# Six query/key blocks between the early wide blocks, a fifth step by seven products in each of these, and the two recurrences side by side, in a hybrid decoder block on one Trainium2 core

## The chip, the cores and the metric

The kernel runs on one core of a Trainium2 chip. The engines that matter here are TensorE (PE, with the loading of its stationary operand shown apart as PEld), VectorE (DVE), ScalarE (ACT), GpSimd (POOL) and SyncE (SP). POOL and SP issue transfers here and do little else. The metric is the time of one execution on the device, in microseconds; the time of a kernel is the median of its runs.

## The reference

One decoder layer over 256 positions of width 2048, all in float32. What is computed:

```python
a = rmsnorm(h, norm_mix_pre)
q_a, k_a, v_a, q_r, f_r, i_r, g_r, gate_a, gate_r = split_columns(a @ w_in)   # 17408 columns
# attention: rotary on q and k, 3 groups (dilations 1, 4, 16) x 8 heads of 128,
# the groups mixed per position by their softmax denominators
attn = ...                                              # 256 x 1024
# recurrence: f = lb + (1 - lb) * sigmoid(f_r); S_t = diag(f_t) S_{t-1} + (1 - f_t) i_t^T;
# o_t = S_t^T silu(q_r_t); RMSNorm per head, times silu(g_r)
r_out = ...                                             # 256 x 1024
y = sigmoid(gate_a) * (attn @ w_attn_branch) + sigmoid(gate_r) * (r_out @ w_hgrn_branch)
h = h + rmsnorm(y @ w_mix_out, norm_mix_post)
gt, up = split(rmsnorm(h, norm_ffn_pre) @ w_ffn_gate_up)
h = h + rmsnorm((silu(gt) * up) @ w_ffn_down, norm_ffn_post)
```

## The kernel before, in words

**Products.** Every float32 operand is split into a high part (ACT copies it to a shorter format) and a low part (DVE subtracts the high part from the operand). A float32 product is then three TensorE products: high by high, high by low, low by high. The weights are streamed from memory once, in units of 1 MB.

**Blocks and steps.** The matrix products are cut into blocks, a block into steps; `seq` is the list of all steps and the main loop (L1833 ff.) emits it in that order. There are three kinds of block:

- A **wide** block (`Wide`, `multiply_wide`) has two times 512 columns and eight steps. A plain step is 24 matmuls of 512 columns. In a step **by seven products** the two-by-two block product is made from seven products in the manner of Strassen, 21 matmuls instead of 24. It costs other engines more: POOL's queue adds a second piece of weights onto the loaded one (L304), DVE makes sums of pieces (`sum`, L405 and L406), ACT their high part (`dh`, L416) and DVE their low part (`dl`, L419). All steps need ACT's high part `w` (L391) and DVE's low part `wl` (L411). After the last step by seven, `gather` (L523 to L532) and `add_up` (L541) put the side products together. The activations' own sums (`pair_sums`, kept as `so`, one for each entry of `X7`) are made once.
- A **W** block has 256 columns, the columns on the rows of the result; four steps of 16 matmuls, half of them 512 and half 256 columns wide. The 24 query and key blocks are of this kind. Their steps need the split at L356 (ACT) and L357 (DVE). When a block has ended, `both_halves` (L274 on ACT, L276 on DVE) takes the result out of its two banks, and `evac_rope` turns it (two rows of L974, then L981 and L982) into a slot `qk`.
- An **N** block is used for the first gate, the branch products and the first FFN block.

**Strings.** `EARLY` holds one string for each of the ten early wide blocks (gates, values, recurrence inputs); an 8 is a plain step, a 7 a step by seven. `EARLY` "87878787" has four sevens.

**Order.** The order of instructions on each engine is that in which the program writes them (a manual schedule): `ahead(n)` writes the split of step n + 2, then come the matmuls of step n, then `advance(evacs)` one piece of the evacuation in work, and `advance_lanes()` one piece of each lane. A lane is a queue of small pieces: the recurrence (two halves of four heads, each eight levels, with `kk` and `fq` products of 8 matmuls on TensorE) and the eight attention heads. An engine does not overtake: an instruction that waits holds all that is written behind it on its engine.

**Slots.** Three slots each for `w` and `wl`, one for `sum`, `dh` and `dl`; three for `raw` (four in some ranges). PSUM has four banks called `acc` and four called `aux`. In the early stage a wide block takes them as two pairs of each: its plain results stand in two pairs of one side, the side products in two pairs of the other, and `FLIP` changes the sides from block to block. In the middle (query/key blocks) a W block takes two single `acc` banks and the lanes take `aux`.

The few lines of the loop that set the order:

```python
        if n >= 2:
            rest = ahead(n)
...
            multiply_wide(st)
...
        advance(evacs)
...
        advance_lanes()
        if type(b) is Block and b.kind == 'W' and n % 5 == 0:
            advance(lanes[1])
```

## Time and profile before

| | us |
|---|---|
| median of 3 runs | 1680.43 |
| lowest and highest | 1678.48, 1681.29 |
| span of the profiled execution, first to last instruction | 1678.2 |
| PE busy in it | 1667.2 (99%) |
| DVE busy | 1452.9 (87%) |
| ACT busy | 950.4 (57%) |

The profiled execution gives its time as its span; the medians of runs lie 2.2 us above it, since a run counts also what lies around the first and the last instruction. In a row of groups the columns are line, engine, operation, output and inputs, their shapes, count, busy time, mean time of one in ns, and idle time of the engine just before them with what ended it. In a timeline row they are start, duration, engine, line, operation, count. Matmuls are pipelined, so that their duration (390 ns for 512 columns) is longer than their spacing: what one costs is read from start to start.

### The profile page before, as it was taken

To read this page: it belongs to the slowest core of one execution; us is meant where nothing else is said; L and a number is where in the kernel's file an instruction comes from. 1 tells how busy PE (TensorE), PEld (TensorE's weight loads), DVE (VectorE), ACT (ScalarE), POOL (GpSimd) and SP (SyncE) were. 2 spreads that over 40 slices of the span, in tenths; PEclk is the share of its full clock that TensorE was granted. 3 is DMA by queue.
4 is the path that set the end of the run, shared out by engine and by line. 5 is a ranking of instruction groups with operands and counts; after the bars stand their busy time and mean duration, and the time that the engine had idled before them with its cause. 6 is when DMAs were issued, how large, how long until landed. Compare 5 with 4: busy or idle time off the path is not lost.

```text
span 1678.2 us, 21503 instructions
## 1 busy us (share of the span) xinstructions
PE 1667.2 (99%) x8046; PEld 1393.7 (83%) x8046; DVE 1452.9 (87%) x1487; ACT 950.4 (57%) x951; POOL 233.6 (14%) x319
## 2 busy tenths in 40 slices
PE   9999999999999999999999999999999999999997
PEld 7888888888888888888888888888888888888886
DVE  6798898889889798877668888999999999899988
ACT  6565555556643544354445565666666666666664
POOL 0011111110133143332200010111111111000100
PEclk9999999999999999999999999999999999999999
DMA  8888888877889899999948857999988999887893
GB/s 280 270 261 257 254 259 259 253 246 226 244 268 308 238 310 297 314 258 299 272 159 257 259 179 249 271 273 278 277 275 277 275 273 278 254 257 241 253 306 104
DMA packets 234841, 434.98 MB, mean 259 GB/s; under 512 B 15312, under 2 KB 65536, under 8 KB 234736
## 3 DMA queue, kind: packets, MB, share of 16 engines
q1 hardware_dynamic: 193616, 337.55, 59.8%
q0 software_dynamic: 38496, 90.13, 23.5%
q10 hardware_dynamic: 2624, 5.92, 1.1%
q8 instruction: 63, 1.03, 0.2%
q14 instruction: 42, 0.34, 0.1%
HBM read 420.44 MB, written 52.43 MB: 282 GB/s over the span
## 4 chain that ended last, share of the span: by engine, by line
PE 85%; DVE 6%; DMA 5%; issue 2%; ACT 1%; SPq 0%; DVEq 0%; ACTq 0%
PE acc L170 52%; PE aux L170 31%; DMA raw<-in_w_in 5%; DVE wl L411 3%; DVE e L541 1%; DVE dl L419 1%; PE aux L1019 0%; DVE sum L406 0%; ACT w L391 0%; DVE e L532 0%; DVE sum L405 0%; PE acc L1512 0%; DVE fz L1644 0%; PE aux L640 0%; PE aux L1512 0%
## 5 line engine op out<-in xcount | busy, mean ns | idle before, releaser
L391 ACT ACTIVATE w<-raw 128x2048 fp32r<-128x2048 f32 x220 | 420.7, 1913 | 231.9 <-issue 83.5
L411 DVE TENSOR_TENSOR wl<-raw,w 128x2048 fp32r<-128x2048 f32 x220 | 501.5, 2286 | 22.2 <-ACT w L391 20.0
L170 PE MATMUL acc<-xT,w 128*128 128x512 f32 (+1 forms) x1536 | 279.3, 339 | 0.0
L356 ACT ACTIVATE w<-raw 128x1024 fp32r<-128x1024 f32 (+1 forms) x159 | 166.6, 1051 | 171.4 <-PE acc L170 130.0
L357 DVE TENSOR_TENSOR w<-raw,w 128x1024 fp32r<-128x1024 f32 (+1 forms) x159 | 193.3, 1216 | 80.9 <-ACT w L356 80.0
L170 PEld LDWEIGHTS acc<-xT,w 128*128 128x128 f32 x1536 | 234.0, 188 | 32.5
L416 ACT ACTIVATE dh<-sum 128x1536 fp32r<-128x1536 f32 x107 | 159.5, 1491 | 165.6 <-PE acc L170 58.4
L419 DVE TENSOR_TENSOR dl<-sum,dh 128x1536 fp32r<-128x1536 f32 x107 | 187.5, 1752 | 23.3 <-ACT dh L416 23.2
L170 PE MATMUL acc<-w,xT 128*128 128x512 f32 x602 | 180.8, 392 | 0.3 <-DVE w L357 0.2
L170 PE MATMUL acc<-w,hT 128*128 128x512 f32 x504 | 152.9, 391 | 0.0
L170 PE MATMUL aux<-w,xT 128*128 128x512 f32 x426 | 138.3, 389 | 0.0
L170 PEld LDWEIGHTS acc<-w,xT 128*128 128x128 f32 x602 | 112.2, 188 | 24.8 <-DVE w L357 1.5
L170 PE MATMUL aux<-w,hT 128*128 128x512 f32 x368 | 122.9, 390 | 0.0
L170 PEld LDWEIGHTS acc<-w,hT 128*128 128x128 f32 x504 | 94.0, 188 | 19.7 <-DVE w L357 0.4
L304 POOL DMA_DIRECT2D raw<-in_w_ffn_gate_up x48 | 42.3, 881 | 377.4 <-DMA raw<-in_w_ffn_gate_up 221.3
L170 PEld LDWEIGHTS aux<-w,xT 128*128 128x128 f32 x426 | 80.0, 188 | 16.5
L170 PE MATMUL aux<-w,a 128*128 128x512 f32 x260 | 83.4, 389 | 0.0
L170 PE MATMUL aux<-wl,xT 128*128 128x512 f32 x213 | 83.1, 390 | 0.0
L170 PEld LDWEIGHTS aux<-w,hT 128*128 128x128 f32 x368 | 69.1, 188 | 14.4
L304 POOL DMA_DIRECT2D raw<-in_w_in x37 | 32.7, 884 | 345.8 <-DMA raw<-in_w_in 240.7
L170 PE MATMUL acc<-wl,xT 128*128 128x512 f32 x205 | 80.0, 390 | 0.3 <-DVE wl L411 0.2
L170 PE MATMUL aux<-w,so 128*128 128x512 f32 x198 | 77.1, 389 | 0.0
(341 smaller groups left out, 3028.1 us busy)
## 6 DMA issues: line engine op xcount, KB each, us to landing
raw<-in_w_in SPq DMA_DIRECT2D x271, 512.0 KB, 6.3
raw<-in_w_ffn_gate_up SPq DMA_DIRECT2D x176, 512.0 KB, 5.0
raw<-in_w_ffn_down SPq DMA_DIRECT2D x88, 512.0 KB, 5.7
sum<-ready SPq DMA_DIRECT2D x25, 768.0 KB, 6.6
ready<-in_w_ffn_gate_up POOLq DMA_DIRECT2D x72, 256.0 KB, 6.9
raw<-in_w_mix_out SPq DMA_DIRECT2D x32, 512.0 KB, 5.3
ready<-ready POOLq DMA_DIRECT2D x50, 256.0 KB, 6.9
raw<-in_w_ffn_gate_up POOLq DMA_DIRECT2D x48, 256.0 KB, 6.0
```

The source lines that it names most:

```text
L170: nc.tensor.matmul(ps, lhsT, rhs, start=start, stop=stop, skip_group_check=True)
L304: nc.gpsimd.dma_start(raw[:, :512], rows, accum_op=OP.add)
L356: nc.scalar.activation(wh[:, k], raw[:, k], AF.Copy)
L357: nc.vector.tensor_sub(wl[:, k], raw[:, k], wh[:, k].bitcast(F32))
L391: nc.scalar.activation(hi, raw, AF.Copy)
L411: nc.vector.tensor_sub(lo, raw, hi.bitcast(F32))
L416: nc.scalar.activation(hi, flat, AF.Copy)
L419: nc.vector.tensor_sub(lo, flat, hi.bitcast(F32))
L541: nc.vector.tensor_add(e, b.bank[keys], e)
```

## The change

1. The activations' sums are made for five pairs of row blocks instead of four (`X7`), and six early blocks (numbers 1 to 6 of 0 to 9) have the string "87877877", five steps by seven instead of four.
2. After each of these six blocks stands one W block, the six query/key blocks of head pair 0. Its two results stand in one pair of PSUM (`side`), on the side on which the block before had its side products, and its evacuation is advanced once more at the block's end. Eighteen W blocks remain in the middle.
3. The recurrence's second half is in lane 1 with a wait of 20 pieces (`LAG`), the first stays in lane 0 with a wait of 2; a third lane is added when the first half has ended. Attention of pair 0 is put in the queue at the end of the early stage.
4. The recurrence's outputs go from PSUM to an SBUF slot (ACT) before their squares are taken; two heads of a pair share one PSUM bank for their output; there are 13 slots `f` instead of 16, and three `qk` slots of their own for pairs 0 and 3.
5. Sums of later weights that are made ahead by DMA (`ready_in`) are also issued in the steps of the added W blocks, and the range with a fourth `raw` slot reaches to the end of the early stage.

```diff
-X7, H7 = tuple(range(4)), tuple(range(5))
+X7, H7 = tuple(range(5)), tuple(range(5))
 MIX = [[(3, 0), (4, 0), (5, 0), (0, 1), (6, 0), (1, 1), (2, 0), (7, 0)],
...
-EARLY = [order(x) for x in ["88878878", "87878787", "87878787", "87878787", "87878787", "87878787", "87878787", "87878787", "88787787", "88787878"]]
+EARLY = [order(x) for x in ["88878878"] + ["87877877"] * 6 + ["87878787", "88787787", "88787878"]]
 FFN = [order(x) for x in ["88878787"] + ["87877877", "87877877", "87877877", "87877877", "87877877", "87877877", "87877877", "87877877", "87877877"]]
...
-N_F = 16
+N_F = 13
+BESIDE, LAG = (1, 2, 3, 4, 5, 6), 20
 WIDE_FQ, FLIP = 2, 1
...
         self.steps = nk // self.per
-        self.banks, self.at = None, {}
+        self.banks, self.at, self.side = None, {}, None
...
         return pool["now"].tile([P, 1024], F32, tag="f", bufs=N_F, name=nm(s))
+
+    def kslot(s):
+        return kp.tile([P, 1024], F32, tag="qk", bufs=3, name=nm(s))
...
         if b.banks is None:
-            b.banks = [acc_bank() for _ in range(2)]
+            if b.side:
+                pair = pair_of(b.side)
+                b.banks = [pair[:, n, :] for n in range(2)]
+            else:
+                b.banks = [acc_bank() for _ in range(2)]
         for s in sides:
...
         for half in range(WIDE_FQ):
-            lanes[0].append(waiting(2, recurrence(half)) if half == 0 else recurrence(half))
+            lanes[half].append(waiting((2, LAG)[half], recurrence(half)))
+        start_attention(0)()
...
             if o == 0:
-                qkT[key] = fslot("qk").rearrange("p (h t) -> p h t", h=4)
+                slot = kslot if key[0] in (0, 3) else fslot
+                qkT[key] = slot("qk").rearrange("p (h t) -> p h t", h=4)
             yield
...
-    attnT, recT = [], []
+    attnT, recT, heads_in = [], [], {}
     def attention(pair, hh):
-        o, head = None, 2 * pair + hh
+        head = 2 * pair + hh
         yield
...
             yield
-            if o is None:
-                o = aux()
+            if pair not in heads_in:
+                heads_in[pair] = aux()
+            o = heads_in[pair][:, hh * S : (hh + 1) * S]
             for c in range(4):
...
         hi, lo, _ = attnT[0](head)
-        nc.scalar.activation(hi, o[:, :S], AF.Copy)
-        nc.vector.tensor_sub(lo, o[:, :S], attnT[0].f32(head))
+        nc.scalar.activation(hi, o, AF.Copy)
+        nc.vector.tensor_sub(lo, o, attnT[0].f32(head))
         done.append(head)
...
         ath = at.rearrange("p (h t) -> p h t", h=4)
-        o = [aux(), aux()]
-        for h in range(4):
-            hs = slice(h * P, (h + 1) * P)
-            mm(o[0][:, hs], ath[:, h, :P], v[:, 0, hs], True, True)
-            mm(o[1][:, hs], a2[:, hs], v[:, 0, hs], True, False)
-            mm(o[1][:, hs], ath[:, h, P:], v[:, 1, hs], False, True)
-        yield
+        o = fslot("o").rearrange("p (b c) -> p b c", b=2)
+        for i in range(2):
+            ps = aux()
+            for h in range(4):
+                hs = slice(h * P, (h + 1) * P)
+                if i == 0:
+                    mm(ps[:, hs], ath[:, h, :P], v[:, 0, hs], True, True)
+                    continue
+                mm(ps[:, hs], a2[:, hs], v[:, 0, hs], True, False)
+                mm(ps[:, hs], ath[:, h, P:], v[:, 1, hs], False, True)
+            yield
+            nc.scalar.activation(o[:, i], ps, AF.Copy)
         ss, rr = small("ss"), small("rr")
...
                 nc.scalar.activation(
-                    junk[:, hs], o[i][:, hs], AF.Square,
+                    junk[:, hs], o[:, i, hs], AF.Square,
                     accum_out=ss[:, 4 * i + h : 4 * i + h + 1],
...
                 nc.vector.scalar_tensor_tensor(
-                    out=rt[:, i, hs], in0=o[i][:, hs], scalar=rr[:, 4 * i + h : 4 * i + h + 1],
+                    out=rt[:, i, hs], in0=o[:, i, hs], scalar=rr[:, 4 * i + h : 4 * i + h + 1],
                     in1=g[:, i, hs], op0=OP.mult, op1=OP.mult,
...
                 values_back(half)
+                if half == 0:
+                    lanes.append(deque())
             yield
...
             post=more_x if half == 0 else None)
+    def rope_block(pair, g, o):
+        col, tab = (COL_K, 2) if o else (COL_Q, 0)
+        then = start_attention(pair) if pair and o and g == 2 else None
+        add("W", w_in, KD, col + 1024 * g + 256 * pair, xT,
+            both_halves(evac_rope((pair, g), o, tab, then), 0))
+
+    ropes = [(pair, g, o) for pair in range(4) for g in range(3) for o in (0, 2)]
     early = [(COL_GA, ("a", 0), AF.Sigmoid), (COL_GB, ("r", 0), AF.Sigmoid),
...
                   pre=({0: lambda: advance(evacs), 1: lambda: flush(lanes[1])}).get(n))
+        if n in BESIDE:
+            rope_block(*ropes.pop(0))
+            blocks[-1].side = "acc" if (n % 2 == FLIP) == False else "aux"
     first_w = len(blocks)
...
         add_wide(w_in, KD, COL_QR + 512 * half, xT, evac_qr(half, start_recurrence(half)))
-    for pair in range(4):
-        for g in range(3):
-            for o, col, tab in ((0, COL_Q, 0), (2, COL_K, 2)):
-                then = start_attention(pair) if o and g == 2 else None
-                add("W", w_in, KD, col + 1024 * g + 256 * pair, xT,
-                    both_halves(evac_rope((pair, g), o, tab, then), 0))
+    for x in ropes:
+        rope_block(*x)
     blocks[first_w].pre = end_early
...
     )
+    ready_in |= {st.unit for st in seq if type(st.block) is Block and st.block.side}
     before = sums_before([
...
     wide = [st.unit for st in seq if type(st.block) is Wide]
-    extra.append(range(wide[0] + N_RAW, wide[0] + 8 * len(early), N_RAW + 1))
+    extra.append(range(wide[0] + N_RAW, blocks[first_w].unit0, N_RAW + 1))
     first = blocks[mix_last + 3].unit0 + N_RAW + 1
...
                 evacs.append(b.evac(b.banks))
+                if b.side:
+                    advance(evacs)
             continue
```

Where this moves instructions, in the order in which an engine has them:

VectorE, the join of early blocks 1 and 2, before. `sum_1167` and `wl_1165` belong to the second step of block 2, `wl_1133` to its first, `e_1191` is the gather of block 1:

```order
L411 TENSOR_TENSOR wl_1133<-raw_999,w_1132 128x2048
L405 TENSOR_TENSOR sum_1167<-raw_1033 128x512
L406 TENSOR_TENSOR sum_1167<-raw_1033,sum_1167 128x1024
L530 TENSOR_TENSOR e_1191<-aux_974,e_1191 128x512
L531 TENSOR_TENSOR e_1191<-aux_984,e_1191 128x512
L532 TENSOR_TENSOR e_1191<-e_1191,aux_984 128x1024
L541 TENSOR_TENSOR e_1191<-acc_931,e_1191 128x1024
L541 TENSOR_TENSOR e_1191<-acc_944,e_1191 128x1024
L411 TENSOR_TENSOR wl_1165<-raw_1033,w_1164 128x2048
```

VectorE, the join of blocks 2 and 3 in the change (lines are some eight higher; L361 is the split of a W step, L419 now makes `wl` and L427 `dl`, L280 takes the added W block `acc_1602` out of PSUM, L984 begins its rotation). `wl_1644` and `wl_1672` belong to the first two steps of block 3:

```order
L549 TENSOR_TENSOR e_1587<-aux_1343,e_1587 128x1024
L361 TENSOR_TENSOR w_1595<-raw_1434,w_1595 128x1024
L361 TENSOR_TENSOR w_1622<-raw_1434,w_1622 128x1024
L419 TENSOR_TENSOR wl_1644<-raw_1469,w_1643 128x2048
L413 TENSOR_TENSOR sum_1674<-raw_1504 128x512
L414 TENSOR_TENSOR sum_1674<-raw_1504,sum_1674 128x1024
L419 TENSOR_TENSOR wl_1672<-raw_1504,w_1671 128x2048
L280 TENSOR_TENSOR sum_1697<-acc_1602,sum_1697 128x256 x2
L984 TENSOR_TENSOR w_1708<-sum_1697,tabs 64x512 x2
L427 TENSOR_TENSOR dl_1703<-sum_1674,dh_1702 128x1536
```

The gather is now followed by two W splits, and the two adds that empty the W block's pair stand behind the low parts and sums of two steps of the next wide block.

TensorE at the same place in the change, in the first step of block 3, which follows the W block: its first side of 12 matmuls goes to `acc_1717`, its second to `acc_1730`:

```order
L171 MATMUL acc_1717<-w_1643,xT_111 128x512 x2
L171 MATMUL acc_1717<-wl_1644,xT_111 128x512
L171 MATMUL acc_1717<-w_1643,xT_111 128x512
L171 MATMUL acc_1730<-w_1643,xT_111 128x512
L171 MATMUL acc_1730<-wl_1644,xT_111 128x512
```

`acc_1730` takes the banks of `acc_1602`, so its first matmul, the thirteenth of the step, waits for the second L280 add.

VectorE in the middle, from one `kk` row of the first recurrence on, up to shortly before the next, before:

```order
L1177 TENSOR_TENSOR kk_3624<-kk_3624,tot_3625 128x64x8
L1181 TENSOR_TENSOR tot_3625<-tot_3625 128x64
L1102 COPY_PREDICATED at_3626<-lmask,aux_3976 128x256x2
L357 TENSOR_TENSOR w_4075<-raw_3891,w_4075 128x1024
L974 TENSOR_TENSOR w_4069<-sum_4040,tabs 64x512
L357 TENSOR_TENSOR w_4106<-raw_3891,w_4106 128x1024
L981 TENSOR_TENSOR sum_4040<-sum_4040,tabs 128x512
L982 TENSOR_TENSOR qk_3916<-sum_4040,w_4069 128x512
L1102 COPY_PREDICATED at_3626<-lmask,aux_4097 128x32x16
L1175 TENSOR_TENSOR fq_2999<-fq_2999,tot_3625 128x32x16
L357 TENSOR_TENSOR w_4135<-raw_3954,w_4135 128x1024
```

The same stretch in the change, where `kk_4676`, `x_4707` and `fq_3948` are the second recurrence's:

```order
L1188 TENSOR_TENSOR kk_4251<-kk_4251,tot_4252 128x64x8
L1192 TENSOR_TENSOR tot_4252<-tot_4252 128x64
L1113 COPY_PREDICATED at_4253<-lmask,aux_4604 128x256x2
L1121 TENSOR_TENSOR x_4707<-kk_4676,fq_3948 128x1024
L361 TENSOR_TENSOR w_4712<-raw_4519,w_4712 128x1024
L984 TENSOR_TENSOR w_4702<-sum_4668,tabs 64x512
L361 TENSOR_TENSOR w_4743<-raw_4519,w_4743 128x1024
L991 TENSOR_TENSOR sum_4668<-sum_4668,tabs 128x512
L992 TENSOR_TENSOR qk_4544<-sum_4668,w_4702 128x512
L1113 COPY_PREDICATED at_4253<-lmask,aux_4734 128x32x16
L1186 TENSOR_TENSOR fq_3624<-fq_3624,tot_4252 128x32x16
L1124 TENSOR_TENSOR fq_3948<-fq_3948,fq_3933 128x1024
```

Two rows of 1024 elements, `x_4707` and `fq_3948`, have come between, and nothing has gone; the next `kk` row follows in both after one W split and the two L276 (L280) adds.

## The prediction

> **What bounds the kernel now.** I read the page's busy times first, then a table by stretches (early wide blocks; query/key blocks in two parts; FFN), then what TensorE's weight loads waited for.
>
> ```profile
> PE 1667.2 (99%) x8046; PEld 1393.7 (83%) x8046; DVE 1452.9 (87%) x1487; ACT 950.4 (57%) x951; POOL 233.6 (14%) x319
> 88.00:465.00 377.00, 376.71 (x1674) 310.89 (x1673) 337.66 (x236) 218.12 (x152) 40.36 (x52) 1.00 0.81 251
> 590.00:790.00 200.00, 199.82 (x1246) 177.46 (x1245) 164.73 (x249) 92.20 (x150) 68.26 (x99) 1.00 1.02 297
> 1100.00:1430.00 330.00, 330.00 (x1486) 272.50 (x1485) 304.14 (x234) 203.53 (x138) 34.39 (x39) 1.00 0.90 275
> ```
>
> The stretches' columns are from:to, length, then busy time of PE, PEld, DVE, ACT, POOL, granted clock, DMA share, GB/s. TensorE is busy everywhere at full clock, so a matmul that goes is worth its spacing and every new wait of TensorE is paid in full. VectorE is second: 337.66 of 377 us in the early stage (90%), 304.14 of 330 (92%) in the FFN. How near the early stage is to the edge is shown by these waits:
>
> ```profile
> PEld acc L170 <- DVE wl L411: 1.3, 3, 0.6
> PEld aux L170 <- DVE wl L411: 0.8, 2, 0.4
> 183.32 2.28 DVE L411 TENSOR_TENSOR wl<-raw,w 128x2048 fp32r<-128x2048 f32 x1
> 184.92 0.61 PE L170 MATMUL acc<-w,xT 128*128 128x512 f32 x2
> 185.34 1.92 ACT L391 ACTIVATE w<-raw 128x2048 fp32r<-128x2048 f32 x1
> 185.52 1.75 DVE L419 TENSOR_TENSOR dl<-sum,dh 128x1536 fp32r<-128x1536 f32 x1
> 185.66 0.19 PEld L170 LDWEIGHTS acc<-wl,xT 128*128 128x128 f32 x1 [0.55 <-DVE wl L411]
> 187.19 2.29 DVE L411 TENSOR_TENSOR wl<-raw,w 128x2048 fp32r<-128x2048 f32 x1
> ```
>
> The first two rows are the weight loads' waits between 100 and 465 us: 2.1 us in five waits, all on a low part `wl`. The others are one of them: `wl` ends at 185.60, and the load that wanted it starts at 185.66. It is the low part of a wide block's second step, which stands behind the gather of the block before.
>
> **What is saved.** Six steps change from 24 matmuls to 21: 18 matmuls fewer.
>
> ```profile
> 459.81 0.39 PE L170 MATMUL acc<-wl,xT 128*128 128x512 f32 x1
> 460.49 0.39 PE L170 MATMUL acc<-wl,xT 128*128 128x512 f32 x1
> 461.17 0.39 PE L170 MATMUL acc<-wl,xT 128*128 128x512 f32 x1
> 471.83 21.76 PE L170 MATMUL acc<-xT,w 128*128 128x512 f32 x124
> ```
>
> Every third matmul is of this form, so six spacings are 461.17 − 459.81 = 1.36 us, 227 ns each: 18 × 0.227 = **4.1 us**. The Trainium skill, "TensorE: Matmul & The Clock Gate", section "Back-to-back issue gap", gives about 131 ns for a sustained stream of such pairs; by it the saving would be an estimated 2.4 us. The rows above say 227 ns, so that figure is not used.
>
> The W block gives the gather 11.2 us of cover (64 matmuls at 21.76/124 = 0.1755 us; a step of 16 is 2.81), so the waits of the kind at 185.66 should go from the six joins. In start to start TensorE lost there 185.66 − 185.15 (the second of the pair at 184.92) − 0.23 = 0.28 us for a wait written as 0.55. All five waits at that proportion are 2.1 × 0.28/0.55 = **1.1 us** saved; bounds 0 and 2.1.
>
> The W blocks' own matmuls, splits and rotations are only moved. So are the loads: the raw weights of six W blocks, on SP's queue, in another place. POOL's queue gets six more accumulating pieces of 256 KB.
>
> **The cost at the join.** Reckon from the W block's first matmul as time zero.
>
> ```profile
> L391 ACT ACTIVATE w<-raw 128x2048 fp32r<-128x2048 f32 x70 | 133.9, 1912 | 74.3 <-issue 50.8 <-PE aux L170 12.2 <-PE acc L170 11.1
> L411 DVE TENSOR_TENSOR wl<-raw,w 128x2048 fp32r<-128x2048 f32 x70 | 160.0, 2286 | 1.8 <-ACT w L391 0.6
> L419 DVE TENSOR_TENSOR dl<-sum,dh 128x1536 fp32r<-128x1536 f32 x35 | 61.4, 1753 | 11.0 <-ACT dh L416 11.0
> L406 DVE TENSOR_TENSOR sum<-raw,sum 128x1024 f32<-128x1024 f32 x34 | 41.7, 1225 | 1.2
> L405 DVE TENSOR_TENSOR sum<-raw 128x512 f32<-128x512 f32 x34 | 23.3, 686 | 18.2 <-DMA raw<-in_w_in 17.9 <-DVE wl L411 0.2
> L276 DVE TENSOR_TENSOR sum<-acc,sum 128x256 f32<-128x256 f32 x34 | 12.7, 414 | 0.0
> L541 DVE TENSOR_TENSOR e<-aux,e 128x1024 f32<-128x1024 f32 x10 | 11.8, 1219 | 0.4
> L531 DVE TENSOR_TENSOR e<-aux,e 128x512 f32<-128x512 f32 x5 | 3.5, 692 | 0.5
> L357 DVE TENSOR_TENSOR w<-raw,w 128x1024 fp32r<-128x1024 f32 x70 | 85.5, 1223 | 22.4 <-ACT w L356 21.9
> L974 DVE TENSOR_TENSOR w<-sum,tabs 64x512 f32<-64x512 f32 x32 | 22.0, 686 | 1.0
> ```
>
> There are three `w` slots, so the high part of the next wide block's first step waits for the slot of the W block's second step, free at 2 × 2.81 = 5.62. From there the chain is fixed by the order rows: high part 1.91, `wl` 2.29, the second step's sums 0.69 + 1.23, its `wl` 2.29, and only then the two adds that empty the W block's pair, 0.83. That ends at 14.86. TensorE ends the W block at 11.23, does the wide step's first side (12 × 0.227 = 2.72) and wants the pair at 13.95: a wait of 0.9 us. With the overlap of neighbours in the rows above (wl starts to dl starts 185.52 − 183.32 = 2.20, and 187.19 is ahead of the high part's end at 187.26) the chain is 14.4 and the wait 0.4. A semaphore's way adds some 0.2 to the start. I take 0.7, six times: **4.2 us**; bounds 6 × 0.4 = 2.4 and 6 × 0.9 = 5.4. Queued behind the waiting matmul are only matmuls; behind the L280 adds on VectorE stands the rotation's first pair, 2 × 0.69, and then `dl` of the second step.
>
> Is VectorE late elsewhere in such a stage? A block with five sevens is 8 × 2.29 + 5 × (1.23 + 0.69 + 1.75) + gather and adds 5.0 (0.69 × 2 + 1.22 × 3) = 41.7 us, the W block 4 × 1.22 + 0.83 + 4 × 0.69 = 8.5, together 50.2, less what neighbours overlap (some 25 times 0.08, 2.20 against 2.29), about 48, in 24 × 0.227 × 3 + 21 × 0.227 × 5 + 11.2 = 51.4 us of TensorE: 93%, where the FFN's same string runs at 92% without a wait. So I cost the fifth seven's sums at nothing; the cover is that margin of some 3 us a stage, of which the `w` slot already takes about 2.6 at the join. Without it, up to the fifth seven's own 0.69 + 1.23 + 1.75 = 3.7 us a stage would show.
>
> **The cost in the middle.** With one recurrence and no attention beside it, VectorE and TensorE meet like this:
>
> ```profile
> L1110 DVE TENSOR_TENSOR x<-kk,fq 128x1024 f32<-128x1024 f32 x2 | 2.4, 1216 | 0.0
> L1113 DVE TENSOR_TENSOR fq<-fq,fq 128x1024 f32<-128x1024 f32 x2 | 2.4, 1220 | 0.0
> 518.44 0.69 DVE L1177 TENSOR_TENSOR kk<-kk,tot 128x512 f32<-128x512 f32 x1
> 519.83 1.89 PE L170 MATMUL aux<-fq,kk 128*128 128x64 f32 x16
> 527.81 0.69 DVE L1177 TENSOR_TENSOR kk<-kk,tot 128x512 f32<-128x512 f32 x1
> 529.99 1.89 PE L170 MATMUL aux<-fq,kk 128*128 128x64 f32 x16
> 537.67 0.68 DVE L1177 TENSOR_TENSOR kk<-kk,tot 128x512 f32<-128x512 f32 x1
> 540.15 1.89 PE L170 MATMUL aux<-fq,kk 128*128 128x64 f32 x16
> 550.40 1.15 PE L170 MATMUL aux<-fq,kk 128*64 128x64 f32 x16
> 559.95 1.05 PE L170 MATMUL aux<-fq,kk 128*128 128x128 f32 x8
> 528.50:538.35 9.85, 9.85 (x64) 8.78 (x63) 9.31 (x15) 3.45 (x5) 4.13 (x6) 1.00 1.10 322
> 538.35:549.18 10.83, 10.83 (x70) 9.67 (x69) 8.36 (x13) 3.85 (x6) 3.92 (x6) 1.00 1.07 305
> 549.18:558.33 9.15, 9.15 (x64) 7.90 (x63) 7.08 (x10) 3.83 (x5) 3.43 (x6) 1.00 1.03 278
> ```
>
> Each product takes the `kk` row ahead of it, with 0.7, 1.5 and 1.8 us to spare; the windows run from one `kk` end to the next. By the order rows of the change the second recurrence begins inside these. Before the product at 529.99 it adds a `kk` row (0.69): `kk` then ends near 529.1, in time. Before that at 540.15 it adds `x` and `fq` of 1024 elements, 1.22 each: 9.31 + 2.44 = 11.75, end 540.9, 0.8 late with the semaphore. The next window gets some 2.6 (0.69 + 1.22 + 0.69): 8.36 + 2.6 = 10.96, end 551.8 against a product one period (10.25 us) after, at 550.4, and 0.8 of delay: 0.6 more. The fourth gets six rows of about 0.69: 7.08 + 4.1 = 11.2, end 563.0 against 560.0 + 1.4 + 0.9 for four products of the second recurrence: 0.7 more. Sum 2.1 us. Later, lane 1's additional advance at every fifth step writes a `kk` row and its product in one step, where TensorE waits for at least that row, 0.69; I take 0.8. Middle: **3.0 us**, bounds 0.7 (that row alone) and 5 (both sums with a third lane's rows of 0.69 ahead of each of four later products). The copies of the recurrence's outputs and the changed slots I cost at nothing: ACT is 92 of 200 us busy there.
>
> **Sum**: −4.1 − 1.1 + 4.2 + 3.0 = **+2.0 us** on a span of 1678.2. The median of the runs lies 2.2 above that span, so 1680.4 + 2.0 = 1682.4. A difference under 0.2% (3.4 us) can't be told from none here.
>
> **Rivals.**
>
> 1. *The saving stays, the waits don't come.* For it: the FFN's 92% without waits, and VectorE's idle 17.9 us for raw weights in L405's row, which says it is often ahead. Against: the slot at 5.62 binds however early VectorE is. It gives −4.1 − 1.1 = −5.2, or 1675.2.
> 2. *VectorE becomes the bound of the middle.* From the first `kk` row of the second recurrence on, each product waits: about five of the first half and four of the second, at 0.9 us (the largest of the waits above), 8 us, beside the same 4.2 at the joins: −5.2 + 4.2 + 8 = +7, or 1687.5. For it: 9.31 of 9.85 us busy with one recurrence. Against: TensorE's waits give VectorE time back, and 82% (164.73 of 200) in the second part of the middle.
> 3. *Raw weights come late.* L405 waits 17.9/34 = 0.53 us each for a load now; with a fifth accumulating piece and made-ahead sums in the W blocks, `sum`, then `dl`, may come 0.5 us late in twelve of the thirty sevens: 6 us more than the forecast, 1688.4. Against: a DMA share of 0.81 there.
>
> That the change saves fewer matmuls than said is excluded by the order rows: 18 fewer on TensorE.
>
> **Chances.** Forecast 0.45, with a range of its own from 1679.5 to 1686 (bounds of the joins and the middle, not all at one end): 0.33 of it within 0.2%, 0.12 above. Rival 1: 0.22, of which 0.19 faster. Rival 2: 0.25, of which 0.22 slower. Rival 3: 0.08, slower. Together faster 0.19, same 0.39, slower 0.42. The range from 1675.0 to 1688.5 takes in most of rivals 1 and 2.
>
> **What would show it.** Right: in the profile after, weight loads of the second pair in the first step after each W block wait on VectorE's L280 adds, about 0.7 us, six times; no `wl` wait at the six joins; `fq,kk` products waiting on L1188 from the second recurrence's start. Wrong: no L280 wait (the chain is shorter than reckoned), or waits on `dl` or on DMA in the early stage, or on the third lane after the first half's end.

## The result: 0.74% slower, and where the time is

The changed kernel took 1692.03 us (median of 5 runs, 1691.05 to 1695.24) against 1680.43 us; the ratio is 1.0074, 95% interval 1.0062 to 1.0087. The profiled execution's span is 1689.3 us, 11.1 more than before. The forecast was 1682.4, with a range to 1688.5.

The page of the changed kernel, its busy times and two groups of matmuls (the last columns are idle time just before them, and what ended it):

```profile
PE 1666.1 (99%) x8028; PEld 1389.8 (82%) x8028; DVE 1475.5 (87%) x1510; ACT 964.9 (57%) x962; POOL 240.3 (14%) x325
L171 PE MATMUL acc<-w,xT 128*128 128x512 f32 x566 | 172.4, 393 | 4.7 <-DVE sum L280 2.6
L171 PE MATMUL aux<-w,xT 128*128 128x512 f32 x390 | 129.5, 390 | 2.6 <-DVE sum L280 2.6
```

The 18 matmuls are gone, and TensorE's busy time is nearly what it was: the 11 us are waits. The view of waits of TensorE in the early stage (48 to 520 us) and in the middle (520 to 800 us), as total, times, longest:

```profile
PE aux L171 <- DVE sum L280: 2.6, 3, 0.9
PE acc L171 <- DVE sum L280: 2.6, 3, 0.9
PE acc L171 <- DVE w L361: 1.2, 1, 1.2
PE acc L171 <- DVE wl L419: 0.9, 1, 0.9
PE acc L171 <- DVE dl L427: 0.8, 1, 0.8
PE aux L171 <- DVE so L565: 0.7, 1, 0.7
PE aux L171 <- DVE wl L419: 0.6, 1, 0.6
...
PE aux L171 <- DVE kk L1188: 1.0, 2, 0.8
PE aux L171 <- DVE attnT L1044: 0.7, 1, 0.7
PE aux L171 <- DVE tot L1192: 0.5, 1, 0.5
PE aux L171 <- ACT pt L1032: 0.3, 1, 0.3
```

Before, the same view had 0.2 us in the early stage and 0.2 in the middle. The six L280 waits are the joins. One of them in the timeline:

```profile
205.91 2.28 DVE L419 TENSOR_TENSOR wl<-raw,w 128x2048 fp32r<-128x2048 f32 x1
207.76 0.39 PE L171 MATMUL acc<-w,xT 128*128 128x512 f32 x1
208.11 0.75 DVE L280 TENSOR_TENSOR sum<-acc,sum 128x256 f32<-128x256 f32 x2
209.00 0.47 PE L171 MATMUL acc<-w,xT 128*128 128x512 f32 x1 [0.85 <-DVE sum L280]
```

VectorE goes from the second step's low part straight to the adds, these end at 208.86, and TensorE goes on at 209.00. From start to start that is 1.24 us where 0.23 is the spacing: 1.0 us lost, where the view says 0.85. By start to start the 11.1 us are made up so:

| place | us |
|---|---|
| 18 matmuls fewer | -4.1 |
| waits at earlier joins that went | -1.0 |
| six joins, the pair waits for L280 | +6.1 |
| start, 53 to 138 us: a W split, `wl`, `so`, `dl` | +3.3 |
| block 5, 331 to 337 us: `wl` and `dl` | +2.1 |
| first matmul of the last early block, 501 us | +0.75 |
| middle, six waits of 0.3 to 1.0 us, less one of 0.3 us that was there before | +3.2 |
| sum, of 11.1 | 10.3 |

Some 0.8 us stands in no row. It is likely the matmul behind each wait: it starts 0.31 to 0.34 us after the one that waited (209.31 after 209.00) where 0.23 is the spacing, and over the waits that came and went before 520 us this makes 0.8 us, an estimate from the start times.

The start and block 5 in the timelines of the changed kernel:

```profile
52.97 0.29 DVE L561 TENSOR_TENSOR s<-f,s 128x128 f32<-128x128 f32 x1
53.18 1.22 DVE L361 TENSOR_TENSOR w<-raw,w 128x1024 fp32r<-128x1024 f32 x1
54.45 0.73 PE L171 MATMUL acc<-w,xT 128*128 128x512 f32 x2 [1.17 <-DVE w L361]
91.24 0.68 DVE L565 TENSOR_TENSOR so<-s,so 128x512 fp32r<-128x512 f32 x1
91.98 0.50 PE L171 MATMUL aux<-w,so 128*128 128x512 f32 x1 [0.71 <-DVE so L565]
...
321.38 0.91 POOL L308 DMA_DIRECT2D raw<-in_w_in  x1 [2.22 <-DVE sum L413]
328.51 0.69 DVE L413 TENSOR_TENSOR sum<-raw 128x512 f32<-128x512 f32 x1 [2.45 <-issue]
332.80 0.50 PE L171 MATMUL acc<-wl,xT 128*128 128x512 f32 x1 [0.91 <-DVE wl L419]
336.67 0.50 PE L171 MATMUL acc<-dl,xT 128*128 128x512 f32 x1 [0.81 <-DVE dl L427]
```

At the start VectorE makes the fifth pair's sums (`s`, L559 to L561) ahead of a W split that TensorE is waiting for, and at 91 us a product wants a `so` that is just made. In block 5 (of 0 to 9; the expectations below call it block 4) VectorE stands for 2.45 us ahead of a `sum`. The profile names no releaser ("issue"), but the last thing that this `sum` needs is the accumulating piece that POOL's queue issued at 321.38. It landed at 328.43, and the `sum` began at 328.51. It was issued among transfers of made-ahead sums.

### The profile page after: what moved, and what is told of

Read it like the earlier page. It is cut to its first block, busy times and chain, and to the rows that moved or that the text cites. A ratio compares the mean times of both kernels' runs of the same rounds, so it can differ in the third digit from the quotient of the medians.

```text
span 1689.3 us, 21523 instructions
## 1 busy us (share of the span) xinstructions
PE 1666.1 (99%) x8028; PEld 1389.8 (82%) x8028; DVE 1475.5 (87%) x1510; ACT 964.9 (57%) x962; POOL 240.3 (14%) x325
## 4 chain that ended last, share of the span: by engine, by line
PE 57%; DVE 5%; issue 1%; ACT 1%; DMA 1%; POOL 0%; DVEq 0%; ACTq 0%; POOLq 0%
PE acc L171 32%; PE aux L171 24%; DVE w L361 1%; DVE at L1113 1%; DMA ready<-ready 0%; DVE w L984 0%; PE aux L1029 0%; DMA ready<-in_w_ffn_gate_up 0%; PE acc L1530 0%; DVE fz L1662 0%; DVE wl L419 0%; PE aux L1530 0%; DVE sum L991 0%; DVE kk L1188 0%; PE aux L636 0%
## 5 line engine op out<-in xcount | busy, mean ns | idle before, releaser
L419 DVE TENSOR_TENSOR wl<-raw,w 128x2048 fp32r<-128x2048 f32 x220 | 501.0, 2286 | 32.9 <-ACT w L399 31.7
L424 ACT ACTIVATE dh<-sum 128x1536 fp32r<-128x1536 f32 x113 | 168.4, 1491 | 148.2 <-PE acc L171 49.7
L361 DVE TENSOR_TENSOR w<-raw,w 128x1024 fp32r<-128x1024 f32 (+1 forms) x159 | 192.8, 1215 | 67.6 <-ACT w L360 67.0
L171 PE MATMUL acc<-xT,w 128*128 128x512 f32 (+1 forms) x1344 | 244.4, 339 | 0.0
L171 PEld LDWEIGHTS acc<-xT,w 128*128 128x128 f32 x1344 | 205.2, 188 | 28.8
L427 DVE TENSOR_TENSOR dl<-sum,dh 128x1536 fp32r<-128x1536 f32 x113 | 198.0, 1753 | 18.7 <-ACT dh L424 18.2
L171 PE MATMUL acc<-w,xT 128*128 128x512 f32 x566 | 172.4, 393 | 4.7 <-DVE sum L280 2.6
L171 PE MATMUL aux<-w,xT 128*128 128x512 f32 x390 | 129.5, 390 | 2.6 <-DVE sum L280 2.6
L171 PEld LDWEIGHTS acc<-w,xT 128*128 128x128 f32 x566 | 105.3, 188 | 29.6 <-issue 4.7
L171 PEld LDWEIGHTS aux<-w,xT 128*128 128x128 f32 x390 | 73.2, 188 | 18.7 <-issue 3.7
L171 PE MATMUL acc<-w,so 128*128 128x512 f32 x210 | 81.7, 389 | 0.0
L171 PEld LDWEIGHTS aux<-w,hT 128*128 128x128 f32 x368 | 69.1, 188 | 14.4
L171 PE MATMUL aux<-dh,so 128*128 128x512 f32 x220 | 78.7, 392 | 0.0
```

What stands on the lines that cost most here:

```text
L171: nc.tensor.matmul(ps, lhsT, rhs, start=start, stop=stop, skip_group_check=True)
L361: nc.vector.tensor_sub(wl[:, k], raw[:, k], wh[:, k].bitcast(F32))
L419: nc.vector.tensor_sub(lo, raw, hi.bitcast(F32))
L424: nc.scalar.activation(hi, flat, AF.Copy)
L427: nc.vector.tensor_sub(lo, flat, hi.bitcast(F32))
```

## The experiments

Each kernel is the changed one with the edit shown, timed against the kernel before on the same chip; ratios are to the kernel before, so that the changed kernel stands at 1.0074. Times of different tables come from different chips; between them, the ratios are to be compared.

### e1: the two adds ahead of the low part

```diff
+            late = late or type(b) is Block and b.side and st.last
...
                 if b.side:
                     advance(evacs)
+                    rest()
```

> The changed kernel with one line moved: in the last step of an added W block the low part of the step after next is written behind the two adds that empty the block's PSUM pair, not ahead of them. Theory (the order of VectorE makes the wait at each join, 1.0 us six times in the changed kernel): the adds end about 2.2 us sooner, before TensorE wants the pair, and the six waits go, 6.1 us; up to 0.3 us a stage comes back as a late dl of the fourth step, which had only 1.0 us to spare behind the wait. 1692.0 - 6.1 + 0 to 2 = 1686 to 1688. Rival (the pair is late because VectorE is late as a whole in a stage with five sevens): the wait only moves to wl or dl, within 1 us of 1692.

Measured: 1690.04 us, ratio 1.0074 (1.0061 to 1.0086). TensorE's waits in its early stage:

```profile
PE aux L171 <- DVE dl L427: 1.8, 6, 0.3
PE acc L171 <- DVE dl L427: 1.6, 4, 0.6
```

All six L280 waits are gone, and ten waits on `dl` are there, two in each of five stages, at the fourth and the fifth step. From start to start most of them cost 0.50 and 0.43 us, all ten 4.9 us, where the six joins cost 6.1. The order of the adds does make the join wait, so the first theory is right on that; but the waits had been covering a VectorE that was late by nearly as much. The rival's "it only moves" is what the time shows.

### e2: four sevens, the added W blocks kept

```diff
-X7, H7 = tuple(range(5)), tuple(range(5))
+X7, H7 = tuple(range(4)), tuple(range(5))
-EARLY = [... ["88878878"] + ["87877877"] * 6 + [...
+EARLY = [... ["88878878"] + ["87878787"] * 6 + [...
```

> The changed kernel with four sevens in the six blocks and four pairs of activation sums, as before the change; the added W blocks and the lanes stay. TensorE has its 18 matmuls back, +4.1 us. Theory (the fifth pair's sums cost 3.7 us in waits between 50 and 140 us, the joins wait whatever the number of sevens): 1692.0 + 4.1 - 3.7 = 1692.4, with six join waits of about 1 us still there and none at 53, 57, 91 us. Rival (the joins wait because of the fifth seven's load on VectorE): the six waits go as well, 1692.4 - 6.1 = 1686.

Measured: 1688.57 us, ratio 1.0060 (1.0048 to 1.0073).

```profile
PE acc L171 <- DVE sum L280: 2.6, 3, 0.9
PE aux L171 <- DVE sum L280: 2.6, 3, 0.9
PE acc L171 <- DVE e L540: 0.6, 1, 0.6
```

The six join waits are there to the hundredth (1.02 start to start), so they do not come from the fifth seven; the waits at 53, 57 and 91 us are gone, and those in block 5 too. By the ratios the fifth seven, which saves 4.1 us of matmuls, makes the changed kernel about 2.3 us slower (0.0014 of 1680), within the overlap of the two intervals.

### e3: the lanes alone

```diff
-BESIDE, LAG = (1, 2, 3, 4, 5, 6), 20
+BESIDE, LAG = (), 20
```

with four sevens as in e2.

> The changed kernel with no added W blocks, four sevens and four pairs of sums: of the change only the lanes are left (recurrences side by side, third lane, 13 f slots, shared bank, copies of o). Theory (two recurrences load VectorE beyond TensorE's step in the middle; it cost the changed kernel about 3 us there): 1680.4 + 2 to 3 = 1682.4 to 1683.4, with fq,kk products waiting on kk. Rival (the middle is slower only because it lost six W blocks): 1680.4, no wait over 0.4 us.

Measured: 1679.03 us, ratio 1.0002 (0.9993 to 1.0011); one wait in the middle, 0.6 us in the view (`tot`, L1192), 0.7 from start to start. Recurrences side by side, the third lane, the copies, the shared bank and 13 slots cost nothing that can be measured here. The theory that two recurrences over-fill VectorE falls, at least for the steps in which the lanes' pieces are written in this kernel.

### e4: no made-ahead sums in the added W blocks

```diff
-    ready_in |= {st.unit for st in seq if type(st.block) is Block and st.block.side}
```

> The changed kernel with no made-ahead sums issued in the added W blocks' steps (they are issued in the middle alone). Theory (the 2.0 us of waits on wl and dl at 331 to 337 us come from one accumulating piece that landed late among the transfers of these sums): these two waits go, 1692.0 - 2.0 = 1690, unless the sums then come late for the FFN. Rival (the piece is late through the fifth seven's own extra transfers): 1692, the waits stay.

Measured: 1697.51 us, ratio 1.0114 (1.0100 to 1.0127). The two waits of block 5 are gone, as the theory has it. The traces show how the piece came to be late. Without these sums POOL issues it at 313.92 us, 7.5 us sooner than in the changed kernel, though it then takes longer to land (8.5 us against 7.0). In the changed kernel a transfer of a made-ahead sum stands ahead of it in POOL's queue, and that one is issued only at 318.07 us, after 5.6 us for which the profile names nothing that POOL waited for. So the piece was issued late; its transfer was not slow.

But without these transfers the sums are still being made when the mix begins (the last is issued at 1034 us, and at 921 in the changed kernel): between 936 and 998 us TensorE waits 0.5 to 2.1 us six times, four times on `wl` and once each on ACT's high part and on `h`, some 7.6 us. They have to be issued early; where, is e10.

### e5 to e8: the slot, the start, the phase, and all three

e5 splits every second step of an added W block into a `wl` slot:

```diff
             rope_block(*ropes.pop(0))
+            for st in seq[-3::2]:
+                st.home = wlow
```

> The changed kernel with every second step of an added W block split into a slot of wl and not of w. Theory (a stage with five sevens and a W block has enough VectorE time in all, but VectorE stands idle some 2.5 us at each join, because the next block's first high part waits for a w slot that the W block holds; the wait on the pair, or in its place the waits on dl, come from that idle time): VectorE has no such gap, the six waits of 1.0 us go and no dl waits come: 6 us less than the changed kernel, ratio to before 1.0074 - 0.0036 = 1.0038. Rival (VectorE is simply over-full in these stages): the gap closes but the waits return on dl or wl, ratio 1.007.

e6 makes the fifth pair's sums during early block 1, which keeps four sevens:

```diff
-... ["88878878"] + ["87877877"] * 6 + ...
+... ["88878878", "87878787"] + ["87877877"] * 5 + ...
-... pair_sums(xT, X7[c - 6 :: 2], x7, ...
+... pair_sums(xT, X7[c - 6 : 4 : 2], x7, ...
-... 1: lambda: flush(lanes[1]) ...
+... 1: lambda: (flush(lanes[1]), lanes[1].append(pair_sums(xT, X7[4:], x7, ...))) ...
```

> The changed kernel with the fifth pair of activation sums made one block later, in early block 1, which goes back to four sevens (three matmuls more, 0.7 us). Theory (3.3 us of waits at 53, 57, 91 and 138 us come from the fifth pair's sums ahead of the first wide blocks' splits): these waits go, 3.3 - 0.7 = 2.6 us less, ratio 1.0074 - 0.0016 = 1.0058; the pair's sums in block 1 may cost up to 1 us there. Rival (those sums cost the same wherever they stand): 1.0074 + 0.0004.

e7 changes the phase of lane 1's additional advance:

```diff
-        if type(b) is Block and b.kind == 'W' and n % 5 == 0:
+        if type(b) is Block and b.kind == 'W' and n % 5 == 4:
```

> The changed kernel with the additional advance of lane 1 at steps whose number leaves 4 on division by 5, and not 0: with 24 steps fewer in the middle ahead of it, that is the phase that the kernel with the lanes alone has in its W blocks. Theory (the middle's 2.6 us more of waits come from pieces of two lanes that meet in one step, which goes by this phase): the waits at 614 to 760 us go down to that kernel's 0.7 us, 2.6 us less, ratio 1.0074 - 0.0016 = 1.0058. Rival (two recurrences over-fill VectorE in any phase, or attention of pair 0 starting sooner does): 1.0074, waits moved but not fewer.

> The three together. If each theory holds and they add up: 6.1 + 2.6 + 2.6 = 11.3 us less than the changed kernel, ratio 1.0074 - 0.0067 = 1.0007, the time of the kernel before within 0.2%; what is then still lost of the 15 matmuls' 3.4 us are the late accumulating piece (2 us) and the wait of 0.75 us where the last early block begins. Rivals: each of the three above that fails leaves its part.

| | us | ratio | interval |
|---|---|---|---|
| e5 slot | 1690.51 | 1.0071 | 1.0059 to 1.0084 |
| e6 start | 1687.42 | 1.0050 | 1.0038 to 1.0063 |
| e7 phase | 1687.63 | 1.0054 | 1.0042 to 1.0067 |
| e8 all three | 1681.78 | 1.0019 | 1.0010 to 1.0028 |

e7's interval just overlaps that of the changed kernel (1.0062 to 1.0087), but its trace is plain. TensorE's waits in the middle of it:

```profile
PE aux L171 <- DVE tot L1192: 0.6, 1, 0.6
PEld aux L171 <- PE acc L171: 0.8, 1, 0.8
```

The same two recurrences, the same third lane, the same 18 W blocks, and 0.6 us of waits where the changed kernel has 2.5: the middle's cost was the step at which an additional piece of lane 1 is written. With 24 steps moved ahead of the middle the count `n % 5` fell on other pieces of the lanes, though that line had not been changed. e6 is plain too: no wait between 48 and 150 us.

e5 is half right. The join waits went from 0.85 to 0.4 us each, not to nothing, and block 5's late piece cost more than it did in the changed kernel, 1.8 us on `wl` in that profile:

```profile
PE acc L171 <- DVE wl L419: 1.8, 1, 1.8
PE acc L171 <- DVE sum L280: 1.2, 3, 0.4
PE aux L171 <- DVE sum L280: 1.2, 3, 0.4
```

From start to start this wait at 332.58 us is 2.1 us, and eight of the matmuls behind it come 0.40 to 0.56 us apart and not 0.23, at a granted clock of 0.53 between 332.6 and 336.2 us: 1.7 us more. So e5 shows what the slot does to the join, and its time shows little.

What holds the join then is read in e8's timeline, on VectorE and ACT:

```profile
193.99 1.13 ACT L825 ACTIVATE e<-e,r1c 128x1024 f32<-128x1024 f32 x1
195.03 3.70 ACT L399 ACTIVATE w<-raw 128x2048 fp32r<-128x2048 f32 x2
196.95 2.29 DVE L419 TENSOR_TENSOR wl<-raw,w 128x2048 fp32r<-128x2048 f32 x1 [1.61 <-ACT w L399]
203.23 0.75 DVE L280 TENSOR_TENSOR sum<-acc,sum 128x256 f32<-128x256 f32 x2
204.12 0.47 PE L171 MATMUL acc<-w,xT 128*128 128x512 f32 x1 [0.39 <-DVE sum L280]
```

With the slot free, the high part at 195.03 still stands behind ACT's gate (L825), which waits for the gather; VectorE loses 1.6 us there and not the 2.1 of the changed kernel (2.08 us ahead of the `wl` at 201.84).

### e9: all four; e10, e11, e12 on top of it

e9 is e8 with e1's edit.

> Slot, start and phase as before, and the two adds that empty the pair written ahead of the low part (the order of the first experiment). Theory (at a join the w slot and the order each hold VectorE back; with both mended neither the pair nor dl is late): the five waits of 0.55 us that were left go, and at most 0.2 us a stage comes back on dl; 2 to 2.8 us less than with three, ratio 1.0019 - 0.0014 = 1.0005. Rival (a stage with five sevens is over-full by about as much): the waits move to dl as in the first experiment, ratio 1.0019.

e10 issues the made-ahead sums of the added W blocks in the last three early blocks:

```diff
-    ready_in |= {st.unit for st in seq if type(st.block) is Block and st.block.side}
-READY_IN = ((-5, 0), (2, 110))
+READY_IN = ((-29, 0), (2, 110))
```

> The same four, and the made-ahead sums that were issued in the added W blocks are issued in 24 steps of the last three early blocks instead. Theory (these sums' transfers make one accumulating piece late in block 4): the wait on dl and wl near 329 us goes, 1.0 to 2 us less than e9; the sums still come in time for mix and FFN. Rival (they make a piece late wherever they stand, or come too late): the wait is found in blocks 7 to 9, or waits of several us in the mix, as with these sums left out.

e11 passes over one pair of each side at early block 7 (`7: lambda: (pair_of("acc"), pair_of("aux"))`).

> The same four, and one pair of each side of PSUM is passed over at early block 7, so that the rotation of pairs stands as before the change where single banks begin. Theory (the wait of 0.75 us near 495 us, at the last early block's first matmul, comes from a single bank that falls on the pair emptied last): this wait goes, 0.7 us less than e9, under what the comparison can tell, but to be seen in the profile. Rival: block 7 now waits for a pair, up to 1 us.

e12 has four sevens in all early blocks and four pairs of sums.

> The same four, with four sevens in the early blocks as before the change (15 matmuls more than e9, 3.4 us on TensorE). Theory (with the joins mended the fifth seven is nearly free, but for the late piece of 1 to 2 us in block 4): e9 + 3.4 - 1 to 2 = 1.5 to 2.5 us more than e9. Rival (the fifth seven costs in waits what it saves): the same as e9.

| | us | ratio | interval |
|---|---|---|---|
| e9 four mends | 1684.00 | 1.0032 | 1.0019 to 1.0044 |
| e10 sums later | 1681.93 | 1.0018 | 1.0009 to 1.0026 |
| e11 pair parity | 1684.38 | 1.0034 | 1.0021 to 1.0046 |
| e12 four sevens | 1679.15 | 1.0000 | 0.9991 to 1.0009 |

TensorE's waits in the early stage of e9, then of e12:

```profile
PE acc L171 <- DVE dl L427: 2.1, 5, 0.9
PE aux L171 <- DVE dl L427: 1.9, 6, 0.3
PE acc L171 <- DVE e L540: 0.6, 1, 0.6
```

```profile
PE acc L171 <- DVE e L540: 0.6, 1, 0.6
PE acc L171 <- DVE wl L419: 0.5, 1, 0.5
```

By the ratios e9, with e1's edit, is 2.2 us slower than e8, which lacks it; the intervals overlap. Both mends of the join do what they should, as e12 shows: with four sevens no wait at a join or on `dl` is left, and the added W blocks cost nothing that can be measured. The one on `wl` is block 5's late piece (0.7 us from start to start at 332 us, behind 3.9 us of VectorE's waiting for its `sum`), so this piece can be late with four sevens too. With five (e9) the waits are on `dl` again, two in a stage, 0.50 and 0.43 us as in e1. That is the rival; by the ratios (1.0032 and 1.0000, intervals apart) the fifth sevens lose 5 us in e9, though they save 15 matmuls, 3.4 us. e10 takes the wait at block 5 from 1.0 to 0.4 us from start to start and gains about 2 us, more than these waits explain; its interval overlaps that of e9. e11 falls: the wait of 0.6 us on `e` that it was to remove is still there (at 497.7 us), a new one of 0.65 us on `dl` came at 392 us, and the one at 399 us grew from 0.49 to 0.74 us. What makes the wait on `e` was not found.

### e13 to e15: the rotation late

Is a stage with five sevens over-full as a whole, or only where the added W block's rotation meets the first sevens? The edit puts the rest of the W block's evacuation into lane 1, four pieces later:

```diff
-                    advance(evacs)
+                    g = b.evac(b.banks)
+                    next(g)
+                    lanes[1].append(waiting(4, g))
                     rest()
```

e13 is e9 with it, e14 is e10 with it, e15 the changed kernel with it and nothing else.

> The four mends of e9, and the added W block's rotation (its four VectorE instructions, 2.7 us; not the adds that empty the pair) written some six steps later, behind the fourth seven's low part. Theory (a stage with five sevens is over-full for VectorE only from the join to its third and fourth step, where adds, rotation and three sevens' sums meet; later in the stage VectorE has time): the ten dl waits of 0.4 to 0.5 us go, about 4.5 us less than e9's 1684.0, so 1679 to 1680, a late piece in block 4 left; at or a little under the kernel before. Rival (over-full over the whole stage): the waits come at the fifth seven or at the gather, 1683 to 1684.

> The same, with the made-ahead sums issued in the last three early blocks and not in the added W blocks, as in e10. Theory: the late piece in block 4 goes too, 0.6 to 1 us less than e13, so 1678 to 1679, ratio to before 0.999 to 1.000. Rival (the sums' transfers do their harm wherever they stand): as e13.

> The changed kernel with the rotation's four instructions late and nothing else. The adds that empty the pair stand where they stood, so the six join waits of 1.0 us should stay, and with them no dl is late; only the late piece in block 4 might be absorbed: ratio 1.0074 - 0.0007 = 1.006 to 1.0075. If the join waits go, the theory that the w slot and the order of the adds make them falls.

| | us | ratio | interval |
|---|---|---|---|
| e13 on e9 | 1690.87 | 1.0068 | 1.0055 to 1.0080 |
| e14 on e10 | 1676.96 | 0.9984 | 0.9975 to 0.9993 |
| e15 alone | 1700.80 | 1.0125 | 1.0111 to 1.0138 |

e10 and e14 differ in the rotation's place alone: ratios 1.0018 and 0.9984, intervals apart. The waits on `dl` are gone; what TensorE still waits for in e14's early stage after 150 us:

```profile
PE aux L171 <- DVE wl L419: 0.7, 1, 0.7
PE acc L171 <- DVE e L540: 0.6, 1, 0.6
```

So the stage is over-full only in its first part, and five sevens can be carried when the made-ahead sums stand elsewhere. e14 is 0.16% faster than the kernel before (0.07 to 0.25%), the only version here that is.

e13 and e14 differ in the place of the made-ahead sums alone, and that is worth 14 us. What VectorE waits for in e13's early stage, and one such wait with POOL's queue:

```profile
DVE sum L413 <- issue: 14.2, 4, 4.2
DVE sum L413 <- DMA raw<-in_w_in: 4.6, 1, 4.6
...
374.65 1.10 POOL L455 DMA_DIRECT2D ready<-in_w_ffn_gate_up  x2 [0.46 <-issue]
376.70 0.53 POOL L455 DMA_DIRECT2D ready<-in_w_ffn_gate_up  x1 [0.94 <-issue]
384.34 0.93 POOL L308 DMA_DIRECT2D raw<-in_w_in  x1 [7.12 <-DMA raw<-in_w_in]
391.21 0.69 DVE L413 TENSOR_TENSOR sum<-raw 128x512 f32<-128x512 f32 x1 [4.02 <-issue]
```

VectorE does nothing for 4.0 us at 387 to 391 us, for a `sum` whose accumulating piece was issued at 384.34 and landed at 391.13. The load under this piece was issued at 372.53, while made-ahead sums were being moved, and took 11.1 us to land; the same load took 9.9 us in e9 and 7.3 in e14. In e9, with the rotation where it was, the waits without a releaser are 3.0 us in two. In e15 the waits for raw weights were 8.7 us (a load named) and 6.0 us (no releaser), the join waits grew (L280: 7.0 us in six, the longest 1.3), and it is by the ratios 8.6 us slower than the changed kernel. My theory expected neither.

e13's rival, waits at the fifth seven, is in part what its `dl` rows show: TensorE waits at the fourth and the fifth. The late loads come first, but VectorE's work has its share, since two of the rotation's four instructions now stand right ahead of these two `dl` (at 395.48 and 402.18 us in this stage). How much each of the two costs was not separated. Which order of transfers makes a load late there, and why so much more when the rotation is late, stays open.

## Why the prediction was wrong, by its own steps

- **What is saved** (4.1 us, and 1.1 us of waits at old joins): as forecast, 4.1 and 1.0. 18 matmuls fewer at 227 ns; none of the `wl` waits at the six joins came back.
- **The join** (4.2 us, 0.4 to 0.9 each): the mechanism, the place and the number of waits were right, the size was 6.1 us, 1.02 each. I took 0.7, near the middle of the two bounds, and the chain ran near the upper one: at the join shown the adds end 14.74 us after the W block's first matmul at 194.12 (14.4 and 14.86 reckoned), TensorE starts 0.14 later and had wanted the pair at 13.87, 0.08 sooner than reckoned. e1, e5 and e12 show both parts of it, the slot and the order of the adds.
- **The fifth seven "at nothing"**: this is the step that failed. In the changed kernel the fifth seven comes with 5.4 us of waits, at the start (3.3) and in block 5 (2.1), and the join waits cover more of the same kind: e1 takes them away and 4.9 us of `dl` waits appear, and in e9 the fifth sevens lose 5 us. Its cover was reckoned as a share, 48 of 51.4 us of VectorE in a stage. The share was right (48.64 of 52.40 us below), and said nothing on when. From the join to the fifth step VectorE has hardly a gap, and the rest of its idle time lies later, where it helps nobody:

```profile
209.00:261.40 52.40, 51.54 (x242) 42.90 (x242) 48.64 (x39) 30.22 (x23) 8.17 (x11) 1.00 0.87 266
251.07:279.35 28.28, 27.70 (x127) 22.47 (x125) 27.40 (x21) 16.15 (x11) 6.40 (x8) 1.00 0.99 293
250.00:278.00 28.00, 28.00 (x129) 23.32 (x128) 27.58 (x20) 15.75 (x12) 4.67 (x6) 1.00 1.00 307
```

  The first row is a whole stage of the changed kernel, the second, of e9, the stretch from a join's first `wl` to the `dl` of the stage's third seven: 27.40 of 28.28 us busy. e14 takes four instructions out of that stretch, 2.7 us, and the waits go. The third row is e14 in about the same 28 us: VectorE is no less busy, 27.58 us, and TensorE does not wait. VectorE ends that `dl` 25.02 us after the join's first `wl` (249.25 to 274.27), and TensorE starts on it at 275.82. What counts is which instructions stand ahead of the `dl`.

  One rival was not tried. Just ahead of the stretch VectorE stands idle for 1.61 us in e9, for a high part that waits behind ACT's gate, as in e8. Whether that time, given back, would also remove the `dl` waits is not shown. The margin of which I let the `w` slot take 2.6 us lost 2.1 there in the changed kernel.

  The FFN was the wrong witness for it, and its row could have said so. In the kernel before, the groups of VectorE between 1100 and 1430 us:

```profile
L419 DVE TENSOR_TENSOR dl<-sum,dh 128x1536 fp32r<-128x1536 f32 x41 | 71.8, 1751 | 9.3 <-ACT dh L416 9.3
L401 DVE TENSOR_TENSOR sum<-raw 128x512 f32<-128x512 f32 x25 | 17.1, 683 | 0.0
```

  41 steps by seven, and sums made on VectorE for 25 of them: in each FFN block two of the five come ready by DMA. The same string is not the same load.
- **The fifth pair of sums at the start** was left out of the sum altogether, though the change names it. It cost 3.3 us, the largest single term that was missed; e2 and e6 show that these waits come and go with it.
- **The middle** (3.0 us, from 2.1 and 0.8): 3.2 measured, but this was luck in part. The product waits on `kk` and `tot` were there (0.68, 0.26 and 0.26 us from start to start for the 0.8, 0.6 and 0.7 reckoned), the step with a `kk` row and its product in one cost 1.00 for 0.8, attention's 1.4 us were not forecast, and a wait of 0.3 us of the kernel before went. The cause was not two recurrences on VectorE: e3 and e7 run them side by side at 0.7 us of waits. It was the phase of one additional advance, which the prediction named as one place of 0.8 us and which decides all but these 0.7 us.
- **The last early block's first matmul**, 0.75 us: not seen. It stands in every kernel here with the added W blocks and not in e3.
- **Rival 3**, raw weights late, got 0.08. It is there in the changed kernel, 2.1 us in block 5 for the 6 it was priced at, and is the largest cost in e13, 14 us against e14. The pieces were the right ones, POOL's accumulating pieces among made-ahead sums of the W blocks; but one came late in the changed kernel, and not twelve. Rival 2's place was wrong: the middle cost 3.2 us and not 8.

The forecast was "no change that can be told", with 0.42 for slower; the time lies 3.5 us above the range. Of the 9.6 us missed, 3.3 are the start, 2.1 block 5, 1.9 the joins and 0.75 the last early block; the rest, some 1.5 us, is small shares and the 0.8 us that no row holds.

## What to carry to other kernels

An engine's share over a stage says whether the work fits, not whether it fits where it stands: walk the instructions from one deadline to the next, with what each of them waits for, and count idle time that lies behind the last deadline as nothing. When a mend of one wait brings waits of nearly the same sum elsewhere (e1), the first was covering the second, and the work has to leave that stretch (e14). A counter like `n % 5` in an order of work is a part of every change that moves the count.

## What the runs showed of the hardware that was not expected

Single loads came late while the stage's means hardly moved. In e13 and e14 the early stage issues the same loads and the same accumulating pieces, the mean DMA share between 150 and 500 us is 0.83 and 0.85, and between 150 and 450 us the median time from issue to landing is 6.3 and 6.4 us for SyncE's loads and 6.7 and 6.8 us for the pieces. Yet with the made-ahead sums among them (e13) `sum` waited 18.8 us for raw weights in five waits, and with these sums in the last three early blocks (e14) 5.2 us in one.

A wait of TensorE can be followed by slow matmuls. Behind the wait at 332.58 us of e5 eight came 0.40 to 0.56 us apart, where the spacing is 0.23, at a granted clock of 0.53 between 332.6 and 336.2 us. In e4, behind waits at 961.26 and 963.59 us, eight came 0.40 to 0.43 us apart, at 0.57 between 963.6 and 967.6 us. The single wait of 2.6 us in e13 (at 398.01 us, from start to start) was followed by none; what makes the difference was not tested.

Before the change, VectorE's waits for raw weights (17.9 us in the L405 row) cost TensorE nothing, since they fell where it was ahead.
